# Six running sums of a filter norm, moved from VectorE to GpSimd

## The chip, the core and the metric

The kernel runs on one core of one Trainium2 chip. Its engines are TensorE (matmuls; the profile calls it PE, and its weight loads PEld), VectorE (DVE), ScalarE (ACT), GpSimd (POOL) and SyncE (SP), which issues transfers; GpSimd issues transfers too. Each engine works through its own queue in order and waits on semaphores for the others. SBUF is the memory on the chip that all of them read; PSUM is where TensorE leaves its products. The metric is the device time of one execution in microseconds (us), the median of several runs.

## The reference, cut to what matters

Two layers of a diffusion backbone over 1024 latent tokens and 256 context tokens of 1024 channels. The first layer has a Hyena part: long convolutions of two orders whose filters come from a small network and are normalised by the sum of their absolute values. That norm is what the change touches:

```python
def hyena_filters(L, w1, b1, freq, w2, b2, w3):
    ...
    h = (h @ w3).reshape(L, 2, HY_ORDER, HY_CH)
    ...
    h = h * jnp.exp(-t01 * deltas)[:, None, None, :]
    h = h / jnp.sum(jnp.abs(h), axis=(0, 1), keepdims=True)
```

`L` is 1024 for the latents and 256 for the context, `HY_ORDER` 2, `HY_CH` 512. Everything else (Fourier groups, projections, neighbourhood attention, two feed-forward blocks) comes later in the kernel.

## The kernel before, in words

Matrix products with full precision are made from pairs: a 32-bit operand is split into a rounded high part (ScalarE, line 287) and the rest (VectorE, line 289), and three products of the parts are added in PSUM. All matmuls of the stage go through line 283.

The work around the change lies in the first 200 us and is made of Python generators that `run` weaves together (lines 1904 to 1929):

- `filter_raw` (from line 579) makes the unnormalised filters of one order. For each of four blocks of 128 positions and two directions it multiplies on TensorE and then, on VectorE, multiplies the product in PSUM by a window (line 613). Each result is a tile of 128x1024 floats, eight for an order.
- `filter_spectrum` (from line 651) transforms them by a DFT on TensorE: four kinds `i`, four blocks `b` each. For every step VectorE adds or subtracts two halves of the raw tiles (lines 674 to 680), the result is split (lines 287 and 289), and GpSimd issues the transfer of a DFT matrix, with a cast from 16 to 32 bits (line 274, called from `cast`, line 338). These matrices go in turn into the buffers named wh, wl and ws, two of each. The finished spectra leave PSUM by ScalarE (line 717).
- `filter_sum` (from line 617) makes the norm beside it, one step of it per block from `i` = 2 on (lines 698 and 699). For the latents each of four steps takes two absolute values of 128x1024 on ScalarE (lines 625 and 626; the raw tiles hold the sum and the difference of the two directions, and the larger of their absolute values is the sum of the directions' own), their maximum on VectorE (line 627), and from the second step on adds it to a running sum (line 629). After that TensorE adds over the 128 positions of a tile by 16 matmuls with a column of ones (line 643), and four small VectorE operations (lines 645 to 648) make the factors that are used hundreds of us later.
- While order 0 is transformed, the raw filters of order 1 are made, and `norms` (line 1855) normalises and modulates the input: on VectorE lines 522 and 525, on ScalarE line 524. Its tiles are what the first projection (`in_proj`, line 744) multiplies next.

The order of each engine's queue is not that of the code alone. Line 2214 opens the kernel so that a planner simulates the time line of all instructions from assumed durations, in priority of the code's order, and fixes each queue's order and the buffer that each tile gets; `issue_after` (line 1915) ties some by hand, none of those that are changed.

```python
    with tile.TileContext(nc, schedule_with_timeline_sim=True) as tc:
```

Of the kernel before, what the change touches and what calls it, by code (L numbers as in the profile page):

```python
# [16 lines left out]
MUL, ADD, SUB, MAX, MIN = ALU.mult, ALU.add, ALU.subtract, ALU.max, ALU.min  # L17
# [183 lines left out]
class Builder:  # L201
# [415 lines left out]
    def filter_sum(self, sq, o, raw):  # L617

        nc = self.nc
        nb = 4 if sq == "l" else 1  # L620
        if sq == "l":
            acc = self.S4()
            for b in range(nb):
                t, x = acc if b == 0 else self.S4(), self.S4()
                nc.scalar.activation(t, raw[(b, 0)], AF.Abs)
                nc.scalar.activation(x, raw[(b, 1)], AF.Abs)
                nc.vector.tensor_tensor(t, t, x, MAX)
                if b:
                    nc.vector.tensor_tensor(acc, acc, t, ADD)
                yield  # L630
            accs = [acc[:, :512], acc[:, 512:]]
        else:
            accs = [self.T(), self.T()]
            for s in (0, 1):
                x = self.T()
                nc.scalar.activation(accs[s], raw[(0, s, 0)], AF.Abs)
                nc.scalar.activation(x, raw[(0, s, 1)], AF.Abs)
                nc.vector.tensor_tensor(accs[s], accs[s], x, MAX)
        yield
        ps = self.PS()  # L640
        for cb in range(4):
            for s in (0, 1):
                self.mm(ps[:, cb * 2:cb * 2 + 1], accs[s][:, cb * P:(cb + 1) * P], self.ones[:, 0:1], s == 0, s == 1)
        nrm, rn, kap = self.C(4), self.C(4), self.C(4)
        nc.vector.tensor_copy(nrm, ps[:, 0:8].rearrange("p (c t) -> p c t", t=2)[:, :, 0])
        nc.vector.tensor_scalar(nrm, nrm, 2.0 * nb * P, None, op0=MUL)
        nc.vector.reciprocal(rn, nrm)
        nc.vector.scalar_tensor_tensor(kap, nrm, 0.5, self.skip[:, o * 4:o * 4 + 4], op0=MUL, op1=MUL)
        self.rn[(sq, o)], self.kap[(sq, o)] = rn, kap
# [1570 lines left out]
```

## Time and profile before

| what | value |
|---|---|
| time before, median of 3 runs | 2981.49 us (2977.06, 2981.49, 2988.88) |
| the profiled execution, its own time | 2974.99 us |
| its span, first to last instruction | 2973.2 us |
| mean granted TensorE clock | 0.990 |
| instructions | 45595 |
| the six adds (line 629), busy | 1206 ns each, 119.8 to 177.5 us |
| the eight maxima (line 627) | 1210 ns each, 108.5 to 175.7 us |

How to read it: one execution was recorded by the hardware's profiler. A row of the time line has the start in us from the span's start, the busy time of the row's instructions together, the engine, the line of the code, the operation, output and inputs by the names of their buffers (s, t and tk are SBUF tiles, c a small SBUF column, ps and pq PSUM, mat a DFT matrix), and the number of instructions merged; in brackets the idle time of the engine just before it and what ended it. Two instructions of one engine can overlap by some 0.1 us, so what one costs its engine is read from start to start. Rows of waits have the sum in us, how many there were, and the longest.

### The profile page before, as it was taken

The numbers are of one execution on the slowest core, as the hardware profiler recorded it, in microseconds if no ns is written. First come the engines' busy times: TensorE is split into PE (matmuls) and PEld (weight loads), VectorE is DVE, ScalarE is ACT, GpSimd is POOL, SyncE is SP. The second block draws the span as 40 slices with busy tenths as digits, with TensorE's granted clock in tenths as the row PEclk, the third lists the DMA queues.
The fourth block names the chain that finished last, engine by engine and source line by source line (L and its number), as shares of the span: only waits on it lengthen the run. The fifth ranks groups of instructions, "written<-read, shape, count | busy, mean of one in ns | idle before, by whom it ended". The sixth has DMA issues, their size and how long they took to land. (4 is left out here: it accounts for less than half of the span.)

```text
span 2973.2 us, 45595 instructions
## 1 busy us (share of the span) xinstructions
PE 2860.4 (96%) x16128; PEld 2389.6 (80%) x16128; DVE 2076.7 (70%) x3988; ACT 1335.7 (45%) x2497; POOL 535.1 (18%) x837
## 2 busy tenths in 40 slices
PE   8899999899999999999999999999999999999997
PEld 3678888888899788788888888888877788888886
DVE  5677787675587777776877536888778887755555
ACT  3453224453455333333445425777765533433442
POOL 2112013353110111113010002233212021102000
PEclk9899999999999999999999999999999999999998
DMA  7774445357456454558886335776856265525663
GB/s 282 238 239 169 166 162 180 117 178 239 155 202 207 170 192 181 192 192 316 304 291 206 127 129 142 174 187 183 226 181 225 85 249 197 188 99 185 224 193 122
DMA packets 314175, 571.89 MB, mean 192 GB/s; under 512 B 84567, under 2 KB 136473, under 8 KB 313947
## 3 DMA queue, kind: packets, MB, share of 16 engines
q1 hardware_dynamic: 255162, 384.38, 40.5%
q0 software_dynamic: 56480, 180.40, 17.0%
q10 hardware_dynamic: 2304, 4.20, 0.4%
q8 instruction: 127, 2.08, 0.3%
q14 instruction: 102, 0.83, 0.1%
HBM read 418.63 MB, written 119.80 MB: 181 GB/s over the span
## 5 line engine op out<-in xcount | busy, mean ns | idle before, releaser
L1283 PE MATMUL ps<-s,s 128*128 128x512 f32 x2028 | 503.3, 390 | 9.8 <-ACT g L1288 3.6
L1283 PEld LDWEIGHTS ps<-s,s 128*128 128x128 f32 x2028 | 379.7, 188 | 93.8 <-ACT g L1288 5.8
L283 PE MATMUL ps<-s,wh 128*128 128x256 f32 (+1 forms) x1780 | 396.0, 328 | 2.7 <-DVE s L720 1.4
L283 PEld LDWEIGHTS ps<-s,wh 128*128 128x128 f32 x1780 | 294.3, 188 | 38.7 <-ACT wh L287 4.0
L283 PE MATMUL pq<-s,wh 128*128 128x512 f32 (+1 forms) x972 | 293.6, 380 | 6.1 <-DVE s L1680 3.6
L287 ACT CAST wh<-ws 128x1024 fp32r<-128x1024 f32 (+1 forms) x139 | 142.3, 1024 | 341.0 <-PE ps L283 158.0
L289 DVE TENSOR_TENSOR wl<-ws,wh 128x1024 fp32r<-128x1024 f32 (+1 forms) x139 | 165.2, 1190 | 138.1 <-ACT wh L287 137.4
L1454 PE MATMUL ps<-s,s 128*128 128x512 f32 (+1 forms) x1000 | 257.9, 383 | 3.2 <-DVE s L289 3.1
L283 PE MATMUL ps<-s,wl 128*128 128x256 f32 (+1 forms) x890 | 257.8, 327 | 2.1 <-DVE wl L289 2.1
L287 ACT CAST s<-s 128x1024 fp32r<-128x1024 f32 (+2 forms) x184 | 168.5, 940 | 187.8 <-DMA s<-d 171.5
L283 PE MATMUL ps<-s,s 128*128 128x64 f16 (+3 forms) x2663 | 215.1, 233 | 15.4 <-DVE st L1752 7.2
L289 DVE TENSOR_TENSOR s<-s,s 128x1024 fp32r<-128x1024 f32 (+2 forms) x162 | 186.7, 1182 | 47.3 <-ACT s L287 44.8
L287 ACT CAST s<-t 128x512 fp32r<-128x512 f32 (+2 forms) x250 | 139.6, 579 | 175.9 <-DVE t L1262 73.2
L1454 PEld LDWEIGHTS ps<-s,s 128*128 128x128 f32 x1000 | 184.5, 188 | 41.1 <-DVE s L289 4.8
L283 PEld LDWEIGHTS pq<-s,wh 128*128 128x128 f32 x972 | 175.7, 189 | 39.3 <-DVE s L1680 5.3
L289 DVE TENSOR_TENSOR s<-t,s 128x512 fp32r<-128x512 f32 (+2 forms) x250 | 164.6, 672 | 49.3 <-ACT s L287 31.1
L1283 PE MATMUL ps<-s,wh 128*128 128x512 f32 x608 | 192.0, 393 | 0.0
L283 PE MATMUL ps<-s,mat 128*128 128x512 f32 x684 | 176.1, 403 | 6.3 <-ACT s L287 5.4
L283 PEld LDWEIGHTS ps<-s,wl 128*128 128x128 f32 x890 | 163.8, 189 | 20.4 <-DVE wl L289 3.6
L283 PE MATMUL pq<-s,wl 128*128 128x512 f32 (+1 forms) x486 | 179.0, 378 | 0.0
L283 PEld LDWEIGHTS ps<-s,mat 128*128 128x128 f32 x684 | 130.2, 193 | 41.1 <-ACT s L287 7.7
L274 POOL DMA_DIRECT2D d<-s x153 | 82.6, 541 | 374.8 <-DVE s L1132 117.1
(384 smaller groups left out, 5647.7 us busy)
## 6 DMA issues: line engine op xcount, KB each, us to landing
s<-d SPq DMA_DIRECT2D x282, 256.0 KB, 3.5
s<-in_down SPq DMA_DIRECT2D x150, 256.0 KB, 4.1
d<-s POOLq DMA_DIRECT2D x137, 256.0 KB, 3.0
d<-tk POOLq DMA_DIRECT2D x98, 256.0 KB, 3.5
s<-in_ada_w POOLq DMA_DIRECT2D x48, 512.0 KB, 4.7
g<-in_bias SPq DMA_DIRECT2D x128, 192.0 KB, 2.7
ws<-in_up SPq DMA_DIRECT2D x44, 512.0 KB, 3.4
d<-g POOLq DMA_DIRECT2D x87, 256.0 KB, 2.9
```

The source lines that it names most:

```text
L274: self.last_ldr = self.nc.gpsimd.dma_start(out, in_).ins
L283: self.nc.tensor.matmul(o, l, r, start=st, stop=sp)
L287: self.last_hi = nc.scalar.copy(hi, src).ins
L289: self.last_lo = eng.tensor_tensor(lo, src, hi.bitcast(F32), SUB).ins
L1283: nc.tensor.matmul(ps, x[:, sl], y, start=first and j == 0 and x is wh and y is xh, stop=j == 3 and x is wl, skip_group_check=True)
L1454: m = nc.tensor.matmul(acc[j][:, c0:c1], x[:, sl], y[:, xs], start=first and k == 0, stop=last and k == 2, skip_group_check=True)
```

## The change

One line. The running sum, for the second, third and fourth step of each of the two orders of the latents' filters, is added by GpSimd; that makes six instructions of 128x1024 floats, in place, both inputs in SBUF. The maximum that each adds stays on VectorE, so GpSimd's add waits for VectorE's maximum, and the ones-matmuls of line 643 wait for GpSimd's last add instead of VectorE's. The context's norm, which has no running sum, is as it was.

```diff
                 nc.scalar.activation(x, raw[(b, 1)], AF.Abs)
                 nc.vector.tensor_tensor(t, t, x, MAX)
                 if b:
-                    nc.vector.tensor_tensor(acc, acc, t, ADD)
+                    nc.gpsimd.tensor_tensor(acc, acc, t, ADD)
                 yield
```

## The prediction

> **What bounds the kernel now.** I read the page's first part, then its chain.
>
> ```profile
> span 2973.2 us, 45595 instructions
> PE 2860.4 (96%) x16128; PEld 2389.6 (80%) x16128; DVE 2076.7 (70%) x3988; ACT 1335.7 (45%) x2497; POOL 535.1 (18%) x837
> ...
> PE 22%; issue 9%; DVE 2%; DMA 1%; ACT 1%; POOL 1%; POOLq 0%; SPq 0%; DVEq 0%; ACTq 0%
> ```
>
> TensorE is busy for 96% of the span; 2973.2 - 2860.4 = 112.8 us is all that it stands idle. Any gain must come out of those 112.8 us, and any loss adds to them. The chain has little to say here: its shares add up to well under half of the span, and in order of time its first piece lies near 1895 us, so it is silent on a change in the first 200 us. I therefore ask the lines that move, and then their stage.
>
> ```profile
> L629 DVE TENSOR_TENSOR s<-s,s x6: 1205/1206/1212, 119.8 to 177.5; 128x1024 f32<-128x1024 f32 x6
> ```
>
> These are the six adds, all between 119.8 and 177.5 us. The view by stretches of the two blocks in which they stand (filters of order 0, then of order 1):
>
> ```profile
> 108.50:141.00 32.50, 23.38 (x81) 17.49 (x80) 32.33 (x54) 14.12 (x26) 3.17 (x6) 0.79 0.65 214
> 158.80:185.00 26.20, 22.28 (x90) 16.07 (x89) 25.20 (x34) 18.45 (x30) 3.27 (x7) 1.00 0.89 299
> ```
>
> After the length come TensorE, weight loads, VectorE, ScalarE, GpSimd. Here, unlike in the kernel as a whole, VectorE is the full engine: 32.33 of 32.50 us and 25.20 of 26.20. TensorE is idle for 9.1 and 3.9 us, and GpSimd for nearly all of it. What TensorE waits for on VectorE from 95 to 190 us (us in total, times, longest):
>
> ```profile
> PE ps L283 <- DVE s L613: 3.9, 1, 3.9
> PE pq L283 <- DVE s L289: 3.1, 1, 3.1
> PE ps L283 <- DVE s L289: 0.9, 3, 0.5
> ```
>
> So the stage is bound by VectorE's queue in places (7.9 us), and a step of VectorE ahead of one of those waits is worth its time one for one. The only other rows of that answer are casts of ScalarE; no wait for a GpSimd transfer is among them.
>
> **The change, part by part. Removed:** six VectorE adds. The time line of order 0's block:
>
> ```profile
> 113.72 1.22 DVE L627 TENSOR_TENSOR s<-s,s 128x1024 f32<-128x1024 f32 x1
> ...
> 114.86 0.48 DVE L522 SCALAR_TENSOR_TENSOR tk<-s,c,s 128x256 f32<-128x256 f32 x1
> ...
> 115.25 0.48 DVE L525 SCALAR_TENSOR_TENSOR s<-t,c,s 128x256 fp32r<-128x256 f32 x1
> ...
> 116.05 1.28 DVE L613 TENSOR_TENSOR s<-ps,s 128x512 f32<-128x512 f32 x2
> ...
> 116.78 1.22 PE L283 MATMUL ps<-s,s 128*128 128x512 f32 x2 [3.94 <-DVE s L613]
> ...
> 119.84 1.21 DVE L629 TENSOR_TENSOR s<-s,s 128x1024 f32<-128x1024 f32 x1
> ...
> 123.23 1.21 DVE L627 TENSOR_TENSOR s<-s,s 128x1024 f32<-128x1024 f32 x1
> ...
> 126.97 1.21 DVE L627 TENSOR_TENSOR s<-s,s 128x1024 f32<-128x1024 f32 x1
> ...
> 129.10 1.21 DVE L629 TENSOR_TENSOR s<-s,s 128x1024 f32<-128x1024 f32 x1
> 130.23 0.68 DVE L289 TENSOR_TENSOR s<-t,s 128x512 fp32r<-128x512 f32 x1
> ...
> 130.97 1.22 PE L283 MATMUL pq<-s,mat 128*128 128x512 f32 x2 [3.14 <-DVE s L289]
> ```
>
> An add takes 1.21 us and, start to start, 1.13 (129.10 to 130.23); six give 6.8 us off VectorE. Two lie ahead of the L289 that TensorE waits for at 130.97; none lies ahead of the L613 at 116.05.
>
> **Added:** six GpSimd adds of 128x1024, a form that the trace lacks. Nearest rows, with both inputs in SBUF:
>
> ```profile
> 206.56 2.54 POOL L593 TENSOR_TENSOR t<-s,s 128x512 f32<-128x512 f32 x2 [20.62 <-DMA s<-in_w]
> ```
> ```profile
> 421.56 0.46 POOL L787 TENSOR_TENSOR s<-s 128x128 f32<-128x128 f32 x1 [2.98 <-DVE s L740]
> ```
>
> 1.27 us for 512 columns and 0.46 for 128: 0.81 / 384 = 2.1 ns a column, so 1.27 + 512 x 0.0021 = about 2.35 us for 1024; twice the 512 form is 2.54, the upper end. I take 2.4, between the two and nearer the line through them. The Trainium skill (GPSIMD Engine Reference, Performance versus the Vector engine) gives 4497 ns for 2048 columns; half of it is an estimate of 2.25 us, and by it the sum below would be about 0.9 us smaller.
>
> **What the add does to VectorE** is the question. Four records show it, first GpSimd's, then VectorE's:
>
> ```profile
> 445.52 2.99 POOL L783 TENSOR_TENSOR s<-s,s 128x512 f32<-128x512 f32 x2 [0.79 <-PE ps L283]
> ```
> ```profile
> 445.85 1.50 DVE L782 TENSOR_TENSOR s<-s,s 128x512 f32<-128x512 f32 x1
> 447.28 0.74 DVE L739 SCALAR_TENSOR_TENSOR s<-ps,c,s 128x511 f32<-128x511 f32 x1
> ```
>
> While GpSimd subtracts, VectorE's L782 with two SBUF inputs takes 1.50 us (a like one takes 0.68: L289 at 130.23), but L739, which has an input in PSUM (ps), keeps its 0.74. The second GpSimd instruction, too, takes 2.99 less the first's 1.3, so 1.7. The two engines take turns at something that operations with two SBUF inputs share. So the change gives back 1.13 us an add and takes up to 2.4. The Trainium skill speaks against the change in the same sense (SBUF — State Buffer, Who interferes with whom): such a VectorE instruction and a GpSimd one that reads SBUF exclude each other, and whichever comes second is blocked until the first is done; the 1.50 us agrees.
>
> Now the sum, with the order of before and the neighbours' inputs as the rows name them. L522, L525, L680, L289 and L627 read two SBUF tiles (they are blocked); L613 reads ps (it isn't).
>
> Order 0. Add 1 may start when the maximum of 113.72 is done, 114.94. L522 is under way to 115.34; the add then holds to 117.75, and L525 of 115.25, with L613 and TensorE's matmul of 116.78 behind it, comes 2.5 us late. The removed add at 119.84 returns 1.13: VectorE is 1.4 late. Add 2 follows the maximum of 123.23 the same way, but an L613 (0.6) runs beside it: 1.8 more, 3.2 late. Add 3 follows the maximum of 126.97: a further 2.2 (its neighbour takes some of it), less 1.13 for the add removed at 129.10. L289 of 130.23, and with it TensorE at 130.97, is 4.3 us late. The last removed add of this order stood behind that wait and returns nothing to TensorE.
>
> Order 1, from these rows:
>
> ```profile
> 164.16 1.21 DVE L627 TENSOR_TENSOR s<-s,s 128x1024 f32<-128x1024 f32 x1
> ...
> 165.95 1.21 DVE L629 TENSOR_TENSOR s<-s,s 128x1024 f32<-128x1024 f32 x1
> ...
> 167.09 0.67 DVE L289 TENSOR_TENSOR s<-tk,s 128x512 fp32r<-128x512 f32 x1
> ...
> 167.69 1.21 DVE L627 TENSOR_TENSOR s<-s,s 128x1024 f32<-128x1024 f32 x1
> ...
> 167.81 3.28 PE L283 MATMUL ps<-s,mat 128*128 128x512 f32 x13 [0.47 <-DVE s L289]
> ...
> 175.69 1.20 DVE L627 TENSOR_TENSOR s<-s,s 128x1024 f32<-128x1024 f32 x1
> ...
> 177.08 0.50 PE L283 MATMUL ps<-s,mat 128*128 128x512 f32 x1 [1.63 <-ACT s L287]
> ...
> 177.48 1.21 DVE L629 TENSOR_TENSOR s<-s,s 128x1024 f32<-128x1024 f32 x1
> ...
> 180.01 0.72 PE L283 MATMUL ps<-s,mat 128*128 128x512 f32 x2 [0.18 <-DVE s L289]
> ...
> 191.05 8.46 PE L283 MATMUL ps<-s,mat 128*128 128x512 f32 x36
> ```
>
> Add 1 puts the L289 of 167.09 late by 2.5 - 1.13 = 1.4 us. Add 2 (after the maximum of 167.69) makes that 3.8, less the second removed add: 2.7 when TensorE waits at 177.08. Add 3, after 175.69, adds 2.4 less the 1.13 of 177.48: TensorE at 180.01 is 4.0 late. At 191.05 begin 36 matmuls in 8.46 us, so TensorE is full from there, and what is lost before stays lost.
>
> Sum: 4.3 + 4.0 = **8.3 us more**. Ends: at worst each add blocks 2.4 and nothing of the 1.13 lies on the path, 6 x 2.4 = 14.4, and 2 x 1.2 more if in each block one buffer that an add gives back 2.4 - 1.2 = 1.2 us later is waited for, 17; at best, without any blocking, -4.6 (a rival below).
>
> **Covers.** The sums are read by 16 matmuls by ones:
>
> ```profile
> 141.11 1.84 PE L283 MATMUL ps<-c,s 128*128 128x1 f32 x16
> ```
>
> Add 3 of order 0 would start near 131.4 and end at 133.8, well ahead. GpSimd issues the DFT matrices in the same queue:
>
> ```profile
> POOL mat L274 <- PE ps L283: 75.0, 19, 11.7
> ```
> ```profile
> DMA to landing us min/median/max: 3.3/4.7/8.0
> ```
>
> Every issue waits for a buffer of TensorE's (19 times, 75.0 us in total), six buffers ahead (two under each of three names) at some 3 us of matmuls each, the 3.28 of the row at 167.81: about 15 us, less 8.0 at worst for the landing. An add in front (2.4) fits; without that cover each would cost its 2.4. The other way round, an add behind an issue that waits the mean 75.0 / 19 = 3.9 us would end by 137.8, still ahead of the 141.11; behind the longest, 11.7, by 145.5, and cost 4.4, less by what TensorE is late itself. I take 0 for both.
>
> **The rivals.**
> *The planner deals other orders, and TensorE loses.* The order on each engine is fixed ahead by a planner that times all instructions; it is not the code's:
>
> ```profile
> 143.11 0.14 DVE L645 COPY c<-ps 128x4 f32<-128x4 f32 x1
> ...
> 148.91 0.16 DVE L647 RECIPROCAL c<-c 128x4 f32<-128x4 f32 x1
> ```
>
> In the code these two stand with only L646 between them; here nearly 6 us lie between, full of other work. A changed add can move what comes after it, in the whole kernel. The price goes by idle time: one more quarter of the 112.8 us is +28 us. It decides from the point where operands of later stages fall behind others in VectorE's full queue, as L613 did at 116.05 (3.94 us in one wait); four such waits reach 0.5%. For it: order 0's block shows TensorE 28% idle when the order fits badly. Against: only six of 45595 instructions change.
> *The same, but TensorE gains:* a quarter less, -28 us, the other side. Against it: TensorE is already at 96%.
> *The relief counts and nothing blocks:* 2.3 off the wait at 130.97, and about 2.3 off the 0.47 + 1.63 + 0.18 at 167.81, 177.08 and 180.01: -4.6. Against it: L782's 1.50.
> *It doesn't do what it says:* VectorE isn't relieved on the path, since the adds run where VectorE happens to read PSUM or to wait; 0.
>
> **How the numbers follow.** The profiled execution took 2974.99 us (span 2973.2 and 1.8 around it); with 8.3 it is 2983.3. The median of before is 2981.49, 6.5 above that execution; on its scale I predict 2981.5 + 8.3 = 2989.8. A measurement of this kernel can tell about 0.5%, 14.9 us (its three runs spread over 11.8): 2966.6 to 2996.4 counts as the same. Chances: the forecast, 0 to +17, 0.38 (0.06 of it past +14.9); planner against 0.37; planner for 0.16; relief 0.06; nothing 0.03. So slower 0.06 + 0.37 = 0.43, the same 0.32 + 0.06 + 0.03 = 0.41, faster 0.16. Cases of both signs hold weight: the forecast's own range is 2981 to 2999; the range for 8 in 10 runs from -20 (2962) to +40 (3022), which leaves out some 0.1 on each side.
>
> **What would show it.** Right: L629 on GpSimd at about 2.4 us, 2.4 to 3.5 where it waits its turn; a VectorE row with two SBUF inputs stretched beside each; VectorE still full in both blocks; TensorE's waits for L613 and L289 longer, and the stage's end (the 36 matmuls of 191.05) some 8 us later, with everything behind it shifted by the same amount. Wrong: unstretched rows beside the adds; a stage that ends earlier; or an equal stage and a difference that arises after 200 us, which would be the planner's.

## The result, and the profile after

The median after the change is 2985.03 us (2977.27 to 2990.16), that of before beside it 2978.18 us (2970.56 to 2988.88), 22 executions of each. The ratio is 1.0023, with a 95% interval of 1.0015 to 1.0031: 6.8 us slower, between 4.5 and 9.2. That is a real loss, but under the 0.5% that the prediction set as its bound. The profiled execution of after took 2977.27 us, the fastest of the 22, so the two spans (2973.2 and 2975.5) understate the difference.

The page of after, its span and the busy time of each engine:

```profile
span 2975.5 us, 45612 instructions
...
PE 2865.3 (96%) x16128; PEld 2396.5 (81%) x16128; DVE 2086.2 (70%) x3982; ACT 1337.4 (45%) x2497; POOL 554.2 (19%) x843
```

GpSimd has 19.1 us more, of which the six adds are 15.5; the other 3.6 lie in its other work and were not followed. VectorE, which lost six instructions, is busy for 9.5 us *more* than before. The six adds as a group (min, median, max in ns):

```profile
L629 POOL TENSOR_TENSOR s<-s,s x6: 2382/2550/2815, 113.0 to 178.8; 128x1024 f32<-128x1024 f32 x6
```

Three of them in GpSimd's time line, the first two of order 0 and the last of order 1:

```profile
113.00 2.52 POOL L629 TENSOR_TENSOR s<-s,s 128x1024 f32<-128x1024 f32 x1 [4.46 <-DVE s L627]
...
123.53 2.41 POOL L629 TENSOR_TENSOR s<-s,s 128x1024 f32<-128x1024 f32 x1 [0.74 <-DVE s L627]
...
178.84 2.69 POOL L629 TENSOR_TENSOR s<-s,s 128x1024 f32<-128x1024 f32 x1 [1.13 <-DVE s L627]
```

What VectorE did beside all six, in its own time line:

```profile
113.23 2.57 DVE L525 SCALAR_TENSOR_TENSOR s<-t,c,s 128x256 fp32r<-128x256 f32 x1
115.73 0.47 DVE L525 SCALAR_TENSOR_TENSOR s<-tk,c,s 128x256 fp32r<-128x256 f32 x1
...
123.31 0.68 DVE L613 TENSOR_TENSOR s<-ps,s 128x512 f32<-128x512 f32 x1
123.91 2.58 DVE L680 TENSOR_TENSOR tk<-s 128x512 f32<-128x512 f32 x1
...
129.28 2.82 DVE L525 SCALAR_TENSOR_TENSOR s<-tk,c,s 128x512 fp32r<-128x512 f32 x1
...
163.58 2.87 DVE L680 TENSOR_TENSOR t<-s 128x512 f32<-128x512 f32 x1
...
171.47 3.49 DVE L289 TENSOR_TENSOR s<-t,s 128x512 fp32r<-128x512 f32 x2
...
179.22 2.87 DVE L525 SCALAR_TENSOR_TENSOR s<-t,c,s 128x512 fp32r<-128x512 f32 x1
```

Read each against its unblocked twin. L525 of 113.23 takes 2.57 us beside the add of 113.00; the next L525, of the same shape, takes 0.47 with no add beside it. L613 of 123.31, which reads PSUM, keeps its 0.68 although the add of 123.53 is running; L680 right behind it reads two SBUF tiles and takes 2.58 (0.68 alone). The stretches are 2.09, 1.90, 2.09, 2.19, 2.22 and 2.14 us: 12.6 us taken, against the 6.8 that the removed adds gave back.

The two blocks as stretches (length, then TensorE, weight loads, VectorE, ScalarE, GpSimd, then granted clock):

```profile
108.50:141.00 32.50, 21.58 (x82) 16.88 (x82) 32.50 (x49) 12.85 (x23) 9.50 (x8) 0.79 0.54 184
158.80:185.00 26.20, 22.68 (x88) 17.00 (x87) 25.02 (x26) 18.03 (x29) 11.29 (x9) 0.91 0.84 274
```

VectorE is as full as before but gets through 49 and 26 instructions instead of 54 and 34. TensorE's waits from 95 to 190 us:

```profile
PE ps L283 <- DVE s L613: 6.0, 1, 6.0
PE ps L283 <- ACT s L287: 4.9, 3, 2.3
PE pq L283 <- DVE s L289: 3.9, 1, 3.9
PE ps L283 <- DVE s L289: 1.9, 1, 1.9
```

The wait for L613 grew from 3.9 to 6.0, those for L289 from 3.1 to 3.9 and from 0.9 to 1.9. To add it up I measure the **stage**: from VectorE's first L678 of order 0, which stands ahead of all that changed, to the start of the 36 matmuls behind which TensorE is full. Before:

```profile
112.06 0.75 DVE L678 SCALAR_TENSOR_TENSOR t<-s,c 128x512 f32<-128x512 f32 x1
```

After, the same instruction, and on TensorE the waits and the end:

```profile
110.04 0.75 DVE L678 SCALAR_TENSOR_TENSOR t<-s,c 128x512 f32<-128x512 f32 x1
```
```profile
116.85 1.22 PE L283 MATMUL ps<-s,s 128*128 128x512 f32 x2 [6.03 <-DVE s L613]
...
132.75 1.22 PE L283 MATMUL pq<-s,mat 128*128 128x512 f32 x2 [3.90 <-DVE s L289]
...
183.41 0.87 PE L283 MATMUL ps<-s,mat 128*128 128x512 f32 x2 [1.93 <-DVE s L289]
...
196.98 8.54 PE L283 MATMUL ps<-s,mat 128*128 128x512 f32 x36
```

Before it is 191.05 - 112.06 = 79.0 us, after 196.98 - 110.04 = 86.9: **7.9 us longer**, and the whole kernel 6.8. So the loss is that of the stage, as far as the interval of the whole (4.5 to 9.2 us) can tell. Each kernel was traced once, so stages come without an interval. (After enters the stage 2.0 us earlier, ahead of anything changed. Comparing plain clock times, 196.98 with 191.05, would show only 5.9.)

### The profile page after: what moved, and what is told of

Read it like the earlier page. It is cut to its first block, busy times and chain, and to the rows that moved or that the text cites. A ratio compares the mean times of both kernels' runs of the same rounds, so it can differ in the third digit from the quotient of the medians.

```text
span 2975.5 us, 45612 instructions
## 1 busy us (share of the span) xinstructions
PE 2865.3 (96%) x16128; PEld 2396.5 (81%) x16128; DVE 2086.2 (70%) x3982; ACT 1337.4 (45%) x2497; POOL 554.2 (19%) x843
## 5 line engine op out<-in xcount | busy, mean ns | idle before, releaser
L289 DVE TENSOR_TENSOR wl<-ws,wh 128x1024 fp32r<-128x1024 f32 (+1 forms) x139 | 165.4, 1191 | 140.9 <-ACT wh L287 140.6
L289 DVE TENSOR_TENSOR s<-s,s 128x1024 fp32r<-128x1024 f32 (+2 forms) x162 | 186.8, 1183 | 46.7 <-ACT s L287 41.7
L289 DVE TENSOR_TENSOR s<-t,s 128x512 fp32r<-128x512 f32 (+2 forms) x250 | 167.1, 683 | 52.5 <-ACT s L287 34.2
```

Source lines behind the costliest of these rows:

```text
L289: self.last_lo = eng.tensor_tensor(lo, src, hi.bitcast(F32), SUB).ins
```

## The experiments

Unless a diff shows another line, each edit stands in the kernel before, at line 629, in place of `nc.vector.tensor_tensor(acc, acc, t, ADD)`. Ratios are to the kernel before, run on the same chip (median 2982.49 us beside the first four kernels, 2978.92 beside the next four, 2981.05 beside the three after them). They come with a 95% interval and need not be the quotient of the two medians. Where the text compares the *order* of an engine between two kernels, it counts lines of the built programs that are in one and not in the other, by code line and buffer name without its number; TensorE's order has 15,988 matmuls. The changed kernel differs from before in 200 of these lines.

**No adds.** How much is the relief alone worth?

```diff
-                    nc.vector.tensor_tensor(acc, acc, t, ADD)
+                    pass
```

> The six adds are left out on both engines (the norm then comes from the first block alone). Blocking theory: VectorE has 6.8 us less in its queue and nothing blocks it, so the start of the 36 matmuls (191.05 us before, 196.98 after) comes 2 to 5 us earlier than before, and the time is 2978 - 4.6, about 2974 (2971 to 2978). It sizes the pure relief. Planner theory (the difference comes from re-dealt orders): another order again, so any value within some 10 us of 2978, with no tie to VectorE's queue.

2978.5 us, ratio 0.9987 (0.9979 to 0.9996): 3.9 us faster. The stage takes 73.6 us, 5.4 less. Its waits:

```profile
PE ps L283 <- DVE s L613: 3.9, 1, 3.9
...
PE ps L283 <- DVE s L289: 3.1, 4, 0.9
```

The L613 wait keeps its 3.9, since no removed add stood ahead of it; the long wait for L289 is gone. So the relief is worth about 4 to 5 us on the path, and the changed kernel loses about 11 to 13 through something that it adds.

**Fills.** The same GpSimd queue, the same waits for the maxima and the same late release of tiles, but work that reads nothing.

```diff
+                    _ = [nc.gpsimd.memset(t, 0.0) for _ in range(2)]
```

> In place of each add GpSimd fills the finished tile t twice with zeros (128x1024 each; it waits for the maximum as the add did, and reads nothing; the running sum is left out). Blocking theory: no VectorE instruction beside a fill is stretched, and the time is that of the kernel without adds, about 2974. Rival theory, that the cost is GpSimd's queue (DFT matrices issued late) and tiles given back late: GpSimd is occupied as before by a queue of waits, so the time is that of the changed kernel, about 2985.

2980.11 us, ratio 0.9990 (0.9980 to 1.0000), stage 73.7. GpSimd's first pair, then VectorE beside it and beside the next:

```profile
113.50 1.96 POOL L629 MEMSET s<- 128x1024 f32 x2 [4.52 <-DVE s L627]
```
```profile
113.75 0.48 DVE L525 SCALAR_TENSOR_TENSOR s<-t,c,s 128x256 fp32r<-128x256 f32 x1
...
122.33 0.68 DVE L680 TENSOR_TENSOR tk<-s 128x512 f32<-128x512 f32 x1
```

The same L525 and L680 that the adds stretched to 2.57 and 2.58 stand at 0.48 and 0.68. Two microseconds of GpSimd in each step, with its wait on VectorE and its tile held as long, cost the stage nothing beside no adds at all (73.7 and 73.6; TensorE's order is the same in both, so the pair also shows how well a stage repeats). That excludes GpSimd's queue and late buffers; what costs is that the add *reads* SBUF. The Trainium skill (SBUF — State Buffer, Who interferes with whom) says just this: a VectorE instruction with two SBUF inputs contends with a GpSimd one that reads SBUF, not with one that only writes. These two kernels agree.

**Each add twice.** If blocking is the cause, its dose should double.

```diff
+                    _ = [nc.gpsimd.tensor_tensor(acc, acc, t, ADD) for _ in range(2)]
```

> GpSimd adds each tile twice (the sums of blocks 2 to 4 count double). Blocking theory: six more blocks of 2.1 us that VectorE gets nothing back for, up to 12.6 us; some of it lies beside work from PSUM, so the stage ends 8 to 13 us later than in the changed kernel and the time is 2985 + 10 = 2995 (2991 to 2999). Planner theory: no dose, near 2985.

3005.43 us, ratio 1.0074 (1.0060 to 1.0088), +22.9; stage 99.9, 12.9 more than with one add. VectorE beside the first pair:

```profile
113.01 2.59 DVE L525 SCALAR_TENSOR_TENSOR s<-t,c,s 128x256 fp32r<-128x256 f32 x1
115.52 2.56 DVE L525 SCALAR_TENSOR_TENSOR s<-tk,c,s 128x256 fp32r<-128x256 f32 x1
```

Now both L525 are stretched, one by each add. The stage is at the upper end of what I had expected (8 to 13), and the whole time is above it: 22.9 - 6.8 = 16 us over the changed kernel where I had 10. A second add gives nothing back, so its full 2.1 us go on the path: six times 2.1 is 12.6, and the stage shows 12.9. The dose is right, the size of the whole was a miss. TensorE's order here is near that of before (42 lines) and not of the changed kernel (204), so the 20.9 us over the stage of before are no re-dealing either.

**Half the columns.**

```diff
+                    nc.gpsimd.tensor_tensor(acc[:, :512], acc[:, :512], t[:, :512], ADD)
```

> GpSimd adds only the first 512 of the 1024 columns (the other half of the running sum is left out). Blocking theory: each add is 1.3 us and blocks about 1.1, what VectorE gets back (1.13): the time is that of before, 2978 (2975 to 2981). Planner theory: the orders are almost those of the changed kernel (86 lines of TensorE's order differ, against 575 between before and changed), so it stays at 2985.

2981.95 us, ratio 1.0001 (0.9989 to 1.0012), stage 82.5. The adds:

```profile
L629 POOL TENSOR_TENSOR s<-s,s x6: 1297/1508/1737, 112.1 to 174.6; 128x512 f32<-128x512 f32 x6
```

As a whole this kernel can't be told from before (within some 3.5 us either way). Its stage is 4.4 us shorter than with the whole add but still 3.5 longer than before; 0.6 of that is a wait of TensorE for the last half add, which the changed kernel doesn't have. This kernel also speaks against the planner: TensorE's order in it differs from the changed kernel's in only 34 lines. Nearly the same dealt order, a stage of 82.5 us instead of 86.9, and 1.0001 instead of 1.0023.

**One order at a time.**

```diff
+                    (nc.vector if o else nc.gpsimd).tensor_tensor(acc, acc, t, ADD)
```

> Only order 0's three adds go to GpSimd. Blocking theory: the wait for L613 is some 2 us longer and the one for L289 near 131 us about 1 us longer, as in the changed kernel; by the prediction's step 4.3 us, so the ratio to before is near 1.0014 (1.0005 to 1.0022). Planner theory: no split by order; either half may carry all of it.

and the other way round:

```diff
+                    (nc.gpsimd if o else nc.vector).tensor_tensor(acc, acc, t, ADD)
```

> Only order 1's three adds go to GpSimd. Blocking theory: nothing changes up to 158 us; then VectorE is blocked three times by about 2.1 us and the 36 matmuls start about 4 us later than before; ratio near 1.0013 (1.0004 to 1.0022). Planner theory: the stage up to 158 us differs too, and the two halves need not add up to the whole.

Order 0 alone: 2984.29 us, 1.0009 (0.9997 to 1.0021), stage 82.7. Order 1 alone: 2983.13, 1.0008 (0.9994 to 1.0023), stage 83.2. Neither whole time tells by itself from no change; the stages do, +3.7 and +4.2, together the +7.9 of the whole change (one trace each, so the exact sum is partly luck). The waits for L613, order 0 alone and then order 1 alone:

```profile
PE ps L283 <- DVE s L613: 6.0, 1, 6.0
```
```profile
PE ps L283 <- DVE s L613: 3.9, 1, 3.9
```

Only with order 0's adds on GpSimd does that wait grow.

**The sum of order 0 later, on VectorE and on GpSimd.** The idea was to put the steps of order 0's sum where TensorE waits for nothing. Line 698, with the adds on VectorE, and then with the adds on GpSimd as well:

```diff
-                if i >= 2:
+                if i >= 2 and (sq == "c" or o == 1):
```

> All adds on VectorE as before, but order 0's whole norm (absolute values, maxima, adds) is put behind its spectrum in the code instead of beside it, so that 4 maxima and 3 adds, 7.9 us, leave the block of 108 to 141 us in which TensorE waits for VectorE. Theory that VectorE's queue is the bound there: the waits for L613 and L289 (3.9 and 3.1 us) shrink, the 36 matmuls start 4 to 8 us earlier and the time is 3 to 7 us under before, ratio 0.9980 (0.9975 to 0.9995). Rival: the moved work falls on 143 to 185 us, where VectorE is as full, and TensorE waits there instead: 1.0000 to 1.0015.

> The kernel of e7 with all six adds on GpSimd. Blocking theory: in the later place order 0's adds still block VectorE by 2.1 us each, but TensorE does not wait for VectorE between 143 and 158 us, so only order 1's adds cost: about 4 us over e7. If every blocked microsecond counted whatever its place, it would be 7 us over e7 or more.

On VectorE: 2977.15 us, 0.9992 (0.9981 to 1.0003), unclear. The premise failed: the planner pulled the moved steps forward to 122 to 141 us, not behind 143. The wait for L613 went, and waits of 4.3 and 4.0 us for L289 took its place; the stage is 79.8 us, no shorter than before. On GpSimd: 2989.88 us, 1.0030 (1.0015 to 1.0045), a miss: some 13 us over its VectorE twin where I had expected 4. The stage is 94.6 us, 14.8 over the twin's, and the twins' orders of TensorE differ in only 28 lines. GpSimd's time line, VectorE's, and TensorE's wait in it:

```profile
130.46 7.13 POOL L629 TENSOR_TENSOR s<-s,s 128x1024 f32<-128x1024 f32 x2 [0.71 <-DVE s L627]
```
```profile
131.37 2.82 DVE L658 TENSOR_TENSOR t<-s,s 1x512 f32<-1x512 f32 x1
...
135.37 2.75 DVE L289 TENSOR_TENSOR s<-t,s 128x512 fp32r<-128x512 f32 x1
```
```profile
PE pq L283 <- DVE s L289: 10.5, 1, 10.5
```

Three adds fell close together ahead of one L289 that TensorE needs, and it waits 10.5 us at once. L658 works on one partition, and it too takes 2.82 us (0.68 before): what counts is that it has two SBUF inputs, not how much it reads.

**The add as an accumulating transfer.** A version without either engine's arithmetic.

```diff
+                    nc.gpsimd.dma_start(acc, t, accum_op=ADD)
```

> The six adds are done by transfers from SBUF to SBUF that add to what they find (issued by GpSimd, 0.53 us of issue each). Theory that a GpSimd instruction reading SBUF is what blocks VectorE: no VectorE row is stretched, VectorE has the 6.8 us less of the kernel without adds, and the stage from L678 to the 36 matmuls is about 74 us as there (73.6; before 79.0); the time is 0.9987 of before (0.9975 to 1.0000). Rival: 512 KB more a transfer that is read and written delay the DFT matrices, TensorE waits for a transfer, and it is at or above 1.0000.

2971.44 us against 2981.05, ratio **0.9966** (0.9953 to 0.9979): about 10 us faster than before, and the fastest kernel here that leaves nothing out. The issues on GpSimd (0.53 us each had been expected), their landing, and VectorE beside the first:

```profile
L629 POOL DMA_DIRECT2D s<-s x6: 880/890/920, 113.7 to 176.8; - x6
...
DMA to landing us min/median/max: 4.5/6.1/8.3
```
```profile
113.66 0.48 DVE L525 SCALAR_TENSOR_TENSOR s<-t,c,s 128x256 fp32r<-128x256 f32 x1
```

No VectorE row is stretched. The landing takes longer than an add but is waited for only once, 1.5 us, at the ones-matmuls. The expected stage of 74 us was a miss: it is 79.1, but with other matmuls in it than before (its last block holds 32 and not 36), so it isn't comparable with the others.

**The sum on TensorE.** The ones-matmuls can add all four maxima themselves, 64 of them in place of 16.

```diff
-            for s in (0, 1):
-                self.mm(ps[:, cb * 2:cb * 2 + 1], accs[s][:, cb * P:(cb + 1) * P], self.ones[:, 0:1], s == 0, s == 1)
+            for s in range(len(accs)):
+                self.mm(ps[:, cb * 2:cb * 2 + 1], accs[s][:, cb * P:(cb + 1) * P], self.ones[:, 0:1], s == 0, s == len(accs) - 1)
```

> No adds: the ones-matmuls take the maxima of all four blocks and sum them in PSUM, 64 rows of 128x1 for an order instead of 16. VectorE has 6.8 us less; TensorE has 48 x 0.115 = 5.5 us more for each order, 11.0 in all, which come together at a place where it is otherwise full. Forecast: 11.0 - 5.4 = 5.6 us more, ratio 1.0019 (1.0005 to 1.0030). If the idle time of TensorE in the stage (9.1 and 3.9 us) took them up: 0.9985.

2993.57 us, 1.0041 (1.0026 to 1.0057), +12.5 where I had +5.6: slower, and by more. The row of order 1:

```profile
188.63 9.07 PE L283 MATMUL ps<-c,s 128*128 128x1 f32 x64
```

That is 0.14 us each, where the 16 of before took 1.84, 0.115 each. With the 64 of order 0 (1.17 + 0.28 + 6.42) they take 16.9 us in place of 3.7: 13.3 more on the one engine without time to spare, less the relief of 3.9 makes 9.4. Of the 3 us left over, 1.4 lie in the 36 matmuls right behind, which take 9.86 us instead of 8.46. The ones-matmuls and these, as stretches (after the clock come DMA share and GB/s):

```profile
188.60:197.60 9.00, 9.00 (x66) 8.96 (x64) 2.70 (x4) 1.62 (x3) 0.00 (x0) 0.78 0.45 129
197.50:207.30 9.80, 9.80 (x38) 7.97 (x39) 1.79 (x5) 6.17 (x9) 0.00 (x0) 0.85 0.44 160
```

The granted clock falls to 0.78 and 0.85 although TensorE is busy all the time.

**One input instead of two.** Does any GpSimd instruction that reads SBUF block for its whole length?

```diff
+                    nc.gpsimd.tensor_scalar(t, t, 2.0, None, op0=MUL)
```

> In place of each add GpSimd multiplies the finished tile t by 2 in place: one SBUF input instead of two (the running sum is left out). If any reading of SBUF by GpSimd blocks VectorE: rows with two SBUF inputs beside it are stretched by its length, and if that is 1 to 2 us the time lies near before's, 0.9995 to 1.0010. If only the second input blocks: nothing is stretched, and the stage and the time are those of the fills, 73.7 us and 0.9990.

2978.95 us, 0.9997 (0.9986 to 1.0009), stage 76.0. GpSimd, and VectorE beside it:

```profile
112.17 2.95 POOL L629 TENSOR_SCALAR s<-s 128x1024 f32<-128x1024 f32 x1 [4.46 <-DVE s L627]
```
```profile
112.38 1.26 DVE L525 SCALAR_TENSOR_TENSOR s<-t,c,s 128x256 fp32r<-128x256 f32 x1
113.56 0.47 DVE L525 SCALAR_TENSOR_TENSOR s<-tk,c,s 128x256 fp32r<-128x256 f32 x1
```

It runs longer than the add, to 115.12, but L525 loses only 0.78 us and its successor nothing, while GpSimd is still at work. Five of the six stretched one row each, by 0.5 to 0.8 us; beside the one that took 6.3 us no row was stretched. So an instruction with one input holds VectorE for a part of its time only. (The stage of 76.0 understates this kernel's loss: the 36 matmuls behind it took 10.08 us at a clock of 0.83, not 8.54.)

**Transfers that add nothing.** The accumulating transfers gain some 6 us more than leaving the adds out does, though neither kernel has an add on VectorE. Is it the accumulation?

```diff
+                    nc.gpsimd.dma_start(x, t)
```

> The same six transfers of 512 KB in GpSimd's queue, but each only copies the maximum over a tile that is no longer needed; nothing is added, so the sum holds the first block alone and the output is not the reference's. The accumulating transfers gave 0.9966 (0.9953 to 0.9979), taking the adds out gave 0.9987 (0.9979 to 0.9996), 2.1 parts in a thousand or about 6 us apart, though neither has an add on VectorE. TensorE's order in this kernel stands much nearer to that of the accumulating transfers than to that of the kernel without adds. If the 6 us come from the orders that the transfers bring about, this kernel is below 0.9980, near 0.9966. If they were the scatter of five runs on one chip, it is near 0.9987 (0.998 to 0.9995). In both cases VectorE's rows with two SBUF inputs keep 0.48, 0.68 and 0.74 us, since nothing runs on GpSimd's arithmetic. Each transfer is issued in about 0.9 us and lands in 4 to 8 us, perhaps sooner than the accumulating ones since it reads one tile and not two.

2969.58 us against 2981.58, ratio 0.9961 (0.9945 to 0.9978). So it wasn't scatter; transfers that add nothing bring the same gain. One ground in that expectation was wrong: the difference in TensorE's order that I had counted was mostly renumbered buffers. With the numbers left out, the kernel without adds differs from the accumulating one in 90 lines and from this one in 116, and these two from each other in 160, so it is no outlier. VectorE's first row beside a transfer, and TensorE's end of the stage:

```profile
113.61 0.48 DVE L525 SCALAR_TENSOR_TENSOR s<-t,c,s 128x256 fp32r<-128x256 f32 x1
```
```profile
185.60 8.54 PE L283 MATMUL ps<-s,mat 128*128 128x512 f32 x36
```

Its L678 stands at 110.4, so the stage takes 75.2 us. By chance this is also the cleanest control of the study: TensorE's order differs from the *changed* kernel's in only 40 lines, VectorE's in 48. Nearly the same order, the same points at which GpSimd is called, no arithmetic on it (and ones-matmuls that need the first block alone): the stage is 86.9 - 75.2 = 11.7 us shorter, and the blocked rows of the changed kernel add up to 12.6.

Much of what the two kernels with transfers gain beyond that lies at the other end of the kernel. When the last output has been issued, GpSimd's queue ends with a DRAIN, and the span ends less than 1.1 us after it. Before and with the copies (ns; the longest of the three is the one meant):

```profile
L2214 POOLq DRAIN  x3: 57/93/9547, 2962.6 to 2972.9; - x3
```
```profile
L2214 POOLq DRAIN  x3: 57/102/2840, 2962.2 to 2965.8; - x3
```

It takes 9.3 to 9.5 us in all twelve kernels without the transfers and 2.8 in both with them. From VectorE's last instruction to the end of the span it is 10.6 to 10.9 us in the twelve, 5.4 in the accumulating kernel and 6.7 in the copying one. So some 5 and 4 us of the gains of 10 and 12 have nothing to do with the sum or with VectorE.

The stages side by side (us, one trace each):

| GpSimd does, per step | one lasts | stage |
|---|---|---|
| nothing, adds on VectorE (before) | | 79.0 |
| nothing, no adds | | 73.6 |
| two fills | 0.95 each | 73.7 |
| a transfer that copies | (issue 0.53) | 75.2 |
| an instruction with one input | 2.8 to 3.1 (one 6.3) | 76.0 |
| half an add | 1.3 to 1.7 | 82.5 |
| **an add (the change)** | 2.4 to 2.8 | 86.9 |
| two adds | median 2.4 each | 99.9 |

From the copy's 75.2, the three kinds of add cost 7.3, 11.7 and 24.7 us, that is 1.2, 1.95 and 4.1 for each of six steps: about 0.8 of the time that GpSimd adds.

## Why the prediction was right, point by point

- **The sign and the size.** 8.3 us were forecast, 6.8 were measured, and 7.9 in the stage.
- **The add's duration.** Taken as 2.4; 2.38 to 2.81, the upper end where it waits its turn, as the L783 rows of before had shown.
- **Two SBUF inputs block, PSUM doesn't.** Right in each row: six stretched, L613 not. An add blocked 2.1 us on average (12.6 / 6), not up to 2.4, since it has run for 0.1 to 0.5 us when the next such row comes. Fills, copies, the half and the double add leave no other reading of the stage.
- **What is given back.** The prediction's relief without blocking was -4.6; the kernels in which nothing blocks (no adds, fills, copies) have stages 5.4, 5.3 and 3.8 us shorter; as a whole the first two are 3.9 and 3.0 us faster (intervals 1 to 6 and 0 to 6), and the third has the shorter end besides.
- **Order 0.** Forecast for TensorE: 2.5 late at L613, 4.3 at L289. Measured from the stage's entry: 116.85 - 116.78 + 2.0 = 2.1, and 132.75 - 130.97 + 2.0 = 3.8; order 0 alone, +3.7.
- **Order 1.** The sum, 4.0, was right (+4.2 alone), but not its make-up. By the steps TensorE would be 8.3 us late at its last wait, 180.01. At 183.41 against 180.01 it has 3.4 + 2.0 = 5.4, only 1.6 more than at the end of order 0. Much of the rest comes behind that wait, from a term that the sum lacked. After and before, the same 11 matmuls:

```profile
183.40:187.60 4.20, 4.19 (x11) 3.32 (x12) 4.20 (x7) 1.23 (x2) 0.46 (x1) 0.59 1.04 357
```
```profile
180.00:182.60 2.60, 2.59 (x11) 2.16 (x12) 2.60 (x5) 0.72 (x1) 0.18 (x1) 1.00 1.14 405
```

  The granted clock is 0.59 instead of 1.00, and that costs 1.6 us. Just ahead of it TensorE had stood for 1.93 us (the row of 183.41 above) and for 1.59:

```profile
180.28 0.50 PE L283 MATMUL ps<-s,mat 128*128 128x512 f32 x1 [1.59 <-ACT s L287]
```

  Before, with waits of 1.63, 0.36 and 0.18 us there, the clock stayed at 1.00. The last 0.9 us of the 7.9 were not followed. Two errors of about the same size cancelled here, so that 4.0 met 4.2 is luck.
- **Covers.** The ones-matmuls didn't wait for the adds, and no GpSimd transfer is among TensorE's waits. Right, and the fills show it without the blocking. (In the half and the double add TensorE does wait for the last add, 0.6 us.)
- **The planner.** It did deal other orders (200 lines of TensorE's), but nothing of the ±28 us came: with nearly the same order as the changed kernel the copies are the fastest of all, and the half add is as fast as before. The 0.53 that the prediction gave to the two planner rivals was too much: a quarter of the idle time is no measure of what swaps of neighbours cost.
- **The chances.** They leaned by a hair to slower by over 0.5%; the time fell in the part of the forecast's own case that lies within it.

**Open.** The two kernels with transfers gain 10 to 12 us, the kernel without adds only 3.9. The shorter DRAIN at the end accounts for some 5 of the accumulating kernel's 6 us of difference, and for 4 of the copying kernel's 8. Why the DRAIN is shorter where GpSimd has issued 664 transfers instead of 658 isn't shown, nor where the copying kernel's other 4 us come from, if they are more than scatter.

## What to carry to other kernels

Before work goes from VectorE to GpSimd, ask what VectorE runs meanwhile: each add with two SBUF inputs held the next VectorE row that has two as well for some 2 us and gave back 1.1, so it was a loss in a block where VectorE was full. Where VectorE reads PSUM no row was held, so there such an add may pay; no run here tried it. Otherwise look for a way without arithmetic, here an accumulating transfer, which held no VectorE row and came out at 0.9966, though about half of that gain came from a shorter end of the kernel. To judge such a change, measure the stage between two fixed instructions. Take as a control the same queue with work that reads nothing, for it tells blocking from queueing, and another whose order of the engines is nearly that of the changed kernel, for it tells blocking from a planner's new order.

## What the runs showed of the hardware that was not expected

- A GpSimd instruction with one SBUF input (2.8 to 3.1 us for 128x1024) stretched a VectorE row with two SBUF inputs by only 0.5 to 0.8 us (five of six; beside the one of 6.3 us none), the add with two inputs, shorter, by 1.9 to 2.2. The Trainium skill's section named above makes no such difference between GpSimd's own forms; here the measurement decides.
- The size of the blocked VectorE row doesn't matter: one of 1x512 waited as long (2.82 us in all) as one of 128x512.
- GpSimd can be the one that waits. In the kernel with each add twice, one add took 5.63 us instead of 2.4: five VectorE rows with two SBUF inputs that began after it, one right behind the other, kept their 0.67 to 0.73 us, and only the sixth was stretched, to 2.87.
- An accumulating transfer of 512 KB within SBUF occupied GpSimd for 0.89 us and landed after 4.5 to 8.3; a plain one took 0.53 and 2.9 to 6.8. While they ran, VectorE's rows with two SBUF inputs kept their 0.48, 0.68 and 0.75 us.
- GpSimd's closing DRAIN took 9.3 to 9.5 us in twelve kernels with 658 transfers issued by GpSimd, and 2.8 us in the two with 664.
- After two waits of under 2 us within five, the granted clock was 0.59 over the next 4.2 us, so these waits of TensorE came to more than their own length. The clock also fell without any wait: to 0.78 over 9.00 us in which TensorE was busy throughout, most of it with 64 matmuls of one column.
